# Operand stores of a feed-forward stage begun by GpSimd's queue instead of SyncE's, and one addition per step made on VectorE instead of GpSimd

## The chip, the cores and the metric

The kernel runs on one core of one Trainium2 chip, as one program in one launch. The core has five engines with an instruction queue each: TensorE (PE) multiplies matrices, VectorE (DVE) and ScalarE (ACT) work on elements, GpSimd (POOL) does elementwise work too, and SyncE (SP) does nothing but begin transfers (DMA). A transfer is begun by an instruction in an engine's queue; the queue runs in program order, so an instruction that waits holds up all that stands behind it in the same queue. The metric is the device time of one execution in microseconds (us), as a median of runs.

## What is computed

The reference is one layer of a decoder over a sequence of 1024 rows of 1024 values, all in float32: an attention and gating mixer with its output projection, a layer norm, and then a feed-forward stage with a second layer norm. The change touches the feed-forward stage alone:

```python
x = layer_norm(ALPHA * x + (1 + g1) * y, ln1_g, ln1_b)       # y: the mixer's output
h = x * (1 + sc2) + sh2                                      # 1024 x 1024
f = (jax.nn.silu(h @ w1) * (h @ w3)) @ w2                    # w1, w3: 1024 x 2816, w2: 2816 x 1024
return layer_norm(ALPHA * x + (1 + g2) * f, ln2_g, ln2_b)
```

## The kernel before

A float32 factor is split into a high part in a rounded format and the rest, the low part: ACT writes the high part (L102; the program calls such tiles wH), and DVE subtracts it from the factor for the low part (L107, wL). Each product of two factors is then three matmuls (high·high, high·low, low·high), issued by `prod` at L1106 in the up stage and at L1333 in the down stage.

**The up stage** makes silu(h@w1)·(h@w3). It uses a scheme that gets a 2×2 block product out of seven products instead of eight, at the price of sums of blocks. It has 22 steps, one for each of 11 pairs of column blocks p and each of the two matrices (w = 0 for w1, 1 for w3). Before a step, `prep1` and `prep2` load two 512-KB pieces of the weight (`raw`, from a pool of four buffers that the pieces of w2 share), build the sums `sa` and `sb` on DVE (L1080 to L1088) and split piece and sums into wH and wL. A step itself is `up_first` (bank pa, its result copied to a tile pt by ACT at L1155), `up_second` (pa goes on), and `up_rest` (banks pb and pcd). In `up_rest` DVE adds pb to the first product (L1175), ACT copies a bank to p5 (L1178), GpSimd adds the first product to it (L1179), and DVE adds the three other banks (L1183, L1187, L1190).

**What is stored.** The down stage needs 77 operand blocks of 128×1024, `comb[i, p]` for seven products i = P1 to P7 and 11 p. They are built during the up stage and go through device memory. The left half comes from `act_out`: h·silu (L1132) and its sums `as` (L1139 to L1146). The right half comes from `w2_sums`: two pieces of w2 are loaded (w2r), four sums are made on DVE (L1047 to L1050, tiles wt), and four of them stored. Each store is one call of `put`, a DMA of 128×512 elements (256 KB). There are 121: 44 of wt, 44 of as, 30 of h and 3 of ea, which are early h. Eleven times, w2_sums runs once every two steps, so that its four puts come in one bunch.

**The down stage** (from about 1008 us) loads the blocks back (`cr`, L1225 and L1226), splits them and multiplies (L1333). Beside that it prepares the residual: the rows r come from device memory (L1290), two vectors lag and lab are loaded as 128×1024 tiles, GpSimd scales each once (L1260, L1262), and DVE makes r·lag (L1294) and adds lab (L1273) for each of eight row tiles.

**What sets the order.** All loads and stores of this stage are issued by SP. The order of the instructions in every queue is laid out ahead of the run by a scheduler, from a model of durations. Tiles wH, sa, sb, wt, as and others come out of one pool of 41 buffers (`B`), nearly all of which long-lived operands hold in this stage. So a new wH gets the buffer of a tile that has just been done with, and where that tile is the source of a put, wH waits until the put has landed. A DMA further waits for the one that was eight before it on the same semaphore lanes (eight lanes for SP's DMAs).

Of the kernel before, what the change touches and what calls it, by code (L numbers as in the profile page):

```python
# [14 lines left out]
MULT, ADD, SUB = ALU.mult, ALU.add, ALU.subtract  # L15
# [28 lines left out]
def hymba_kernel(ctx, tc, x, c, w_ada, b_ada, w_in, cmp_pos, cmp_w1, cmp_w2, vn_g, vn_b, w_s, b_s,  # L44
# [4 lines left out]
    V_, P_, A_ = nc.vector, nc.gpsimd, nc.scalar  # L49
    dma = nc.sync.dma_start  # L50
# [21 lines left out]
    def H2(dt=F32, tag="h2"):  # L72
        return sml.tile([128, 512], dt, tag=tag, name=nm_(tag), bufs=NPT if tag == "pt" else 4)

    def G(nm="g"):
        return psg.tile([128, 512], F32, tag="g", name=nm_(nm), bufs=3)

    def S2(nm="s"):
        return pss.tile([128, 2, 512], F32, tag="s", name=nm_(nm))
# [445 lines left out]
    for a in range(2):  # L525
        p = G("pws")
# [434 lines left out]
    for n in range(NC_ + TL):  # L961
# [26 lines left out]
        while eq and (n >= eq[0][0] or n == NC_ + TL - 1):  # L988
            _, i, kv = eq.pop(0)
# [39 lines left out]
    comb = {(i, p): dram.tile([128, 1024], F32, name=f"comb{i}_{p}") for i in DN for p in range(NP)}  # L1029

    def put(i, p, side, src):

        dma(comb[i, p][:, side * 512:side * 512 + 512], src)

    def w2_blk(p, z):
        return w2[(2 * p + z) * 128:(2 * p + z + 1) * 128]
# [3 lines left out]
    def w2_sums(p):  # L1040

        rw = [RAW("w2r") for _ in range(2)]
        for z in range(2):
            load(rw[z], w2_blk(p, z), 8)
        (b11, b12), (b21, b22) = [halves(r) for r in rw]
        (t1, t3), (t2, t4) = halves(B("wt")), halves(B("wt"))
        V_.tensor_tensor(t1, b12, b11, SUB)  # L1047
        V_.tensor_tensor(t3, b22, b12, SUB)
        V_.tensor_tensor(t2, b22, t1, SUB)
        V_.tensor_tensor(t4, b21, t2, SUB)  # L1050
        for i, b in zip(("P4", "P5", "P6", "P7"), (t4, t1, t2, t3)):
            put(i, p, 1, b)
# [48 lines left out]
    def prod(o, a, b, start=True, early=False):  # L1101

        for i in range(4):
            (lh, ll), (rh, rl) = a[i], b[i]
            for n, (x_, y_) in enumerate(((lh, rh), (lh, rl), (ll, rh))):
                r = nc.tensor.matmul(o, x_, y_, start=start and i == 0 and n == 0, stop=i == 3 and n == 2, skip_group_check=not start)  # L1106
                if early:
                    in_order(r)
            if early:
                ticks[0] += 1  # L1110
                if ticks[0] in TR:
                    advance_h2()
        marks.append(r)
# [11 lines left out]
    def act_out(p, w, q, c):  # L1125

        if w == 0:
            s = silu[p, q] = room(p, q)
            A_.activation(s, c, AF.Silu)
        else:  # L1130
            s = silu.pop((p, q))
            V_.tensor_tensor(s, s, c, MULT)  # L1132
            a = acts.setdefault(p, {})
            a[q] = s
            if q != 1:
                put({0: "P1", 2: "P2", 3: "P4"}[q], p, 0, s)
            if q == 1:
                (s1, s3), (s2, s4) = a["s"] = halves(B("as")), halves(B("as"))
                V_.tensor_tensor(s1, a[1], a[3], ADD)  # L1139
                V_.tensor_tensor(s3, a[0], a[1], SUB)  # L1140
                V_.tensor_tensor(s2, s1, a[0], SUB)
                for i, t in (("P5", s1), ("P6", s2), ("P7", s3)):
                    put(i, p, 0, t)
            if q in (1, 2) and 2 in a and "s" in a:
                _, (s2, s4) = a["s"]
                V_.tensor_tensor(s4, a[2], s2, SUB)  # L1146
                put("P3", p, 0, s4)
# [10 lines left out]
    def up_second(p, w, a, early=False):  # L1158
        prod(a, ops[p, w]["A12"], BOP["B21"], False, early)
        act_out(p, w, 0, a)  # L1160
# [8 lines left out]
    def up_rest(p, w, a):  # L1169
        o, p1 = ops[p, w], keep.pop((p, w))  # L1170
        b = (OT if (2 * p + w) % 2 else G)("pb")
        cd = S2("pcd")
        c, d = cd[:, 0, :], cd[:, 1, :]
        prod(b, o["S2"], BOP["T2"])
        V_.tensor_tensor(p1, p1, b, ADD)  # L1175
        prod(c, o["S1"], BOP["T1"])
        p5 = H2(F32, "pt")
        A_.activation(p5, c, AF.Copy)  # L1178
        P_.tensor_tensor(p5, p5, p1, ADD)  # L1179
        if a is not None:  # L1180
            up_second(p, w, a)
        prod(d, o["S3"], BOP["T3"])
        V_.tensor_tensor(p5, p5, d, ADD)  # L1183
        act_out(p, w, 3, p5)
        prod(c, o["S4"], BOP["B22"], False)
        p7 = H2(F32, "pt")
        V_.tensor_tensor(p7, p1, c, ADD)  # L1187
        act_out(p, w, 1, p7)
        prod(d, o["A22"], BOP["T4"], False)
        V_.tensor_tensor(p1, p1, d, ADD)  # L1190
        act_out(p, w, 2, p1)
# [51 lines left out]
    for n, s in enumerate(steps):  # L1243
        if n < 2:
            continue
        if n + 1 < len(steps):
            if n + 1 >= NE:
                prep1(*steps[n + 1])
            prep2(*steps[n + 1])
        if n in W2:  # L1250
            w2_sums(W2[n])
        if n == len(steps) - 1:
            down_start()
        up_rest(*s, up_first(*s) if n >= NE else None)
# [182 lines left out]
```

## Time and profile before

| what | before |
|---|---|
| median of three runs | 1239.02 us (1238.83 to 1240.66) |
| profiled execution, its own time | 1242.85 us |
| span in its profile | 1241.1 us |
| mean granted clock of TensorE in the span | 0.994 |
| TensorE busy | 1201.1 us (97%) |
| VectorE busy | 951.0 us (77%) |
| ScalarE busy | 555.3 us (45%) |
| GpSimd busy | 246.9 us (20%) |

The median is compared with the median of the changed kernel; the rows come from the one profiled execution, which was 3.83 us longer than the median and has 1.75 us outside its span. Rows of a timeline give start, duration, engine, line, operation, output<-input and shape; in square brackets stands the idle time of the engine before the instruction and what ended it. SPq is SP issuing a DMA. "x2" says that two instructions in a row were joined in one line of the answer. The granted clock (PEclk) is a share of TensorE's full speed.

### The profile page before, as it was taken

Reading aid. Unit: us, or ns where it says so; the run is one execution under the profiler, and the core shown is the slowest. Engines: PE = TensorE matmul, PEld = TensorE weight load, DVE = VectorE, ACT = ScalarE, POOL = GpSimd, SP = SyncE. Lnnn points to the kernel's source line nnn. Section 1 sums busy time; section 2 is a strip of 40 time slices with the busy share of each in tenths; the row PEclk is TensorE's granted clock in tenths of the full one; section 3 lists DMA queues with packets and bytes.
Section 4 is the critical chain, followed back from the end, with each engine's and each line's share of the span. In section 5 each row is a group of like instructions: output and inputs, shape, how many; then the busy total and the mean of one; then the engine's idle time right before and its main releaser. Section 6 shows DMA issues by size and latency. Waiting matters only on the chain.

```text
span 1241.1 us, 16779 instructions
## 1 busy us (share of the span) xinstructions
PE 1201.1 (97%) x5908; PEld 1000.4 (81%) x5908; DVE 951.0 (77%) x1696; ACT 555.3 (45%) x1023; POOL 246.9 (20%) x277
## 2 busy tenths in 40 slices
PE   7999999999999999999989899999999999999996
PEld 5888888888888888888868788888788877888885
DVE  6568798599889997867587577776667759877886
ACT  5653223398889995044333233232322323453420
POOL 0022026075556673100001100000010000000011
PEclk9999999999999999999999999999999999999999
DMA  9624549110000006534053555546544469786741
GB/s 351 245 59 124 164 118 260 48 69 1 2 1 2 1 2 219 161 130 134 28 176 104 153 165 157 162 130 240 163 153 150 134 224 344 232 279 208 240 148 68
DMA packets 125690, 178.35 MB, mean 144 GB/s; under 512 B 16420, under 2 KB 74916, under 8 KB 125607
## 3 DMA queue, kind: packets, MB, share of 16 engines
q1 hardware_dynamic: 125606, 177.30, 44.6%
q8 instruction: 46, 0.75, 0.3%
q14 instruction: 38, 0.30, 0.1%
HBM read 135.06 MB, written 40.11 MB: 141 GB/s over the span
## 4 chain that ended last, share of the span: by engine, by line
PE 87%; DVE 7%; DMA 2%; issue 2%; ACT 1%; POOL 0%; DVEq 0%; ACTq 0%; POOLq 0%
PE pcd L1106 17%; PE pa L1106 10%; PE px L1333 8%; PE py L1333 7%; PE pt L128 4%; PE pb L1106 4%; PE ps L730 2%; PE ps L732 2%; PE pwo L92 2%; PE pwo L96 2%; PE pwo L95 2%; PE ot L774 2%; PE ot L773 2%; PE pv L92 1%; PE pv L95 1%
## 5 line engine op out<-in xcount | busy, mean ns | idle before, releaser
L102 ACT ACTIVATE wH<-cr 128x1024 fp32r<-128x1024 f32 x77 | 81.5, 1061 | 115.4 <-DMA cr<-combP 48.9
L743 POOL TENSOR_SCALAR P<-P,ast,gate 128x640 f32<-128x640 f32 (+7 forms) x128 | 99.5, 784 | 66.6 <-DVE ast L742 43.0
L107 DVE TENSOR_TENSOR wL<-cr,wH 128x1024 fp32r<-128x1024 f32 x77 | 94.0, 1233 | 23.7 <-ACT wH L102 23.0
L1179 POOL TENSOR_TENSOR pt<-pt,pt 128x512 f32<-128x512 f32 x20 | 30.9, 1545 | 396.6 <-ACT pt L1178 191.0
L107 DVE TENSOR_TENSOR pt<-pt,pt 128x512 fp32r<-128x512 f32 (+1 forms) x148 | 99.8, 682 | 7.1 <-ACT pt L102 6.3
L676 ACT ACTIVATE P<-P,ast 128x640 f32<-128x640 f32 (+7 forms) x128 | 93.9, 735 | 2.0 <-DVE ast L675 1.5
L102 ACT ACTIVATE pt<-pt 128x512 fp32r<-128x512 f32 (+1 forms) x148 | 87.2, 592 | 16.2 <-PE pt L128 13.5
L1106 PE MATMUL pa<-h2H,wH 128*128 128x512 f32 x192 | 77.0, 401 | 5.3 <-ACT wH L102 5.3
L102 ACT ACTIVATE wH<-raw 128x1024 fp32r<-128x1024 f32 (+2 forms) x43 | 44.5, 1040 | 81.3 <-DMA combP<-wt 69.7
L128 PE MATMUL pt<-ident,P 128*128 128x128 f32 x528 | 79.0, 272 | 0.2 <-DVE pt L107 0.2
L1106 PE MATMUL pa<-h2L,wH 128*128 128x512 f32 x192 | 76.2, 397 | 0.0
L1106 PE MATMUL pa<-h2H,wL 128*128 128x512 f32 x192 | 75.8, 395 | 0.0
L128 PEld LDWEIGHTS pt<-ident,P 128*128 128x128 f32 x528 | 65.0, 140 | 12.9 <-issue 0.5
L107 DVE TENSOR_TENSOR wL<-raw,wH 128x1024 fp32r<-128x1024 f32 (+2 forms) x43 | 51.4, 1199 | 30.9 <-ACT wH L102 29.0
L1333 PE MATMUL px<-wH 128*128 128x512 f32 x176 | 68.4, 395 | 3.1 <-DVE h L1406 2.2
L1333 PE MATMUL px<-wL,wH 128*128 128x512 f32 x176 | 69.3, 394 | 1.8 <-DVE wL L107 1.8
L1106 PE MATMUL pcd<-wH,wH 128*128 128x512 f32 x176 | 68.8, 391 | 1.5 <-DVE h L1132 0.8
L1333 PE MATMUL px<-wH,wL 128*128 128x512 f32 x176 | 69.3, 394 | 0.0
L1106 PE MATMUL pcd<-wL,wH 128*128 128x512 f32 x176 | 68.5, 389 | 0.0
L1106 PE MATMUL pcd<-wH,wL 128*128 128x512 f32 x176 | 68.5, 389 | 0.0
L773 PE MATMUL ot<-pt,V 128*128 128x512 f32 x132 | 59.8, 453 | 0.0
L730 PE MATMUL ps<-KH,Q 128*128 128x512 f32 (+2 forms) x192 | 57.2, 354 | 1.0 <-DVE ast L675 0.9
(300 smaller groups left out, 3396.9 us busy)
## 6 DMA issues: line engine op xcount, KB each, us to landing
raw<-in_w SPq DMA_DIRECT2D x46, 512.0 KB, 5.6
cr<-combP SPq DMA_DIRECT2D x44, 512.0 KB, 4.4
ada<-in_w_adaT SPq DMA_DIRECT2D x32, 512.0 KB, 6.1
w2r<-in_w SPq DMA_DIRECT2D x22, 512.0 KB, 4.3
combP<-wt SPq DMA_DIRECT2D x44, 256.0 KB, 5.2
combP<-as SPq DMA_DIRECT2D x44, 256.0 KB, 2.1
cr<-combP SPq DMA_DIRECT2D x33, 256.0 KB, 4.5
cr<-in_w SPq DMA_DIRECT2D x33, 256.0 KB, 5.0
```

Of the source, the lines that this page charges most:

```text
L92: a = nc.tensor.matmul(o, lh[0], rh[0], start=start, stop=False)
L95: nc.tensor.matmul(o, lh[0], rh[1], start=False, stop=False)
L102: A_.activation(o, i, AF.Copy)
L107: return V_.tensor_tensor(o, i, f(h), SUB)
L128: nc.tensor.transpose(out=p[:, j * 128:(j + 1) * 128], in_=src(j), identity=ident)
L676: A_.activation(P, P, AF.Exp, scale=-1.0, bias=nm, accum_out=den)
L730: nc.tensor.matmul(o, Q(h, hf)[:, qs], KH(br - 1, kv, kf)[:, ks], start=True, stop=False)
L743: P_.tensor_scalar(P, P, st[:, 2, hh:hh + 1], gcol(i, h, br), MULT, MULT)
L773: nc.tensor.matmul(ot, vs, hl[0], start=False, stop=False)
L1106: r = nc.tensor.matmul(o, x_, y_, start=start and i == 0 and n == 0, stop=i == 3 and n == 2, skip_group_check=not start)
L1179: P_.tensor_tensor(p5, p5, p1, ADD)
L1333: lastm[0] = nc.tensor.matmul(o, x_[:, ts_], y_[:, 512:1024], start=not cont and p == 0 and n == 0, stop=p == NP - 1 and n == 2, skip_grou ...
```

## The change

Two lines change. In `put` all 121 stores are begun by GpSimd's queue instead of SP's. In `up_rest` the addition at L1179 is done by DVE: 20 instructions, one for each of the 20 steps that use `up_rest`.

```diff
     def put(i, p, side, src):
 
-        dma(comb[i, p][:, side * 512:side * 512 + 512], src)
+        P_.dma_start(comb[i, p][:, side * 512:side * 512 + 512], src)
...
         p5 = H2(F32, "pt")
         A_.activation(p5, c, AF.Copy)
-        P_.tensor_tensor(p5, p5, p1, ADD)
+        V_.tensor_tensor(p5, p5, p1, ADD)
         if a is not None:
             up_second(p, w, a)
```

(`dma` is SP's `dma_start`, P_ is GpSimd, V_ is DVE.) GpSimd's DMAs get eight semaphore lanes of their own (DMASW; SP's are DMAHW). As the scheduler lays the queues out anew and buffers are handed out in another order, instructions move on all engines. Three places are shown. Numbers behind tile names tell instances apart.

ACT at the end of the step before p = 2, where TensorE idles at 686 to 690 us in the trace; in brackets are the semaphores on which an instruction waits. wH_7080 is the high part of the next step's first piece. Before:

```order
L102 ACTIVATE wH_6946<-sa_6942 128x1024 [waits DVE_49]
L102 ACTIVATE wH_6952<-sb_6943 128x1024 [waits DMAHW4_49,DMAHW5_49,DVE_49,Activation_49]
L102 ACTIVATE w_6956<-raw_6940 128x512 [waits DMAHW2_49,DMAHW3_49,DMAHW0_49,Activation_49]
L1129 ACTIVATE h_7045<-pt_7015 128x512 [waits DMAHW3_49,DVE_49]
L102 ACTIVATE wH_7080<-raw_7078 128x1024 [waits DMAHW3_49,DMAHW0_49,DMAHW4_49,DVE_49,Activation_49]
L1155 ACTIVATE pt_7116<-pa_7103 128x512 [waits PE_49]
```

And now:

```order
L102 ACTIVATE wH_6946<-sa_6942 128x1024 [waits DVE_49]
L102 ACTIVATE wH_6952<-sb_6943 128x1024 [waits DVE_49,PE_49]
L1129 ACTIVATE h_7045<-pt_7015 128x512 [waits DMASW4_49,DVE_49]
L102 ACTIVATE w_6956<-raw_6940 128x512 [waits DMASW1_49,DMAHW4_49,DMASW0_49,Activation_49]
L102 ACTIVATE wH_7080<-raw_7078 128x1024 [waits DMAHW7_49,PE_49]
L1155 ACTIVATE pt_7116<-pa_7103 128x512
```

Before, wH_7080 waited for two puts of wt (lanes 3 and 4), whose source had its buffer; now it has another buffer and waits for its own raw piece (lane 7) and a past product. The same holds at the step before p = 7, where TensorE idles at 882 to 884 us. At both places the first product with this wH also stands 12 matmuls later in TensorE's queue than before.

TensorE at the step before p = 3, which stands for six alike (it is at 732 us in the trace): pa_7539 is the next step's first bank, pcd_7272 a bank of the step that is ending. Rows with - are the order before, rows with + the order now:

```order
 L1106 MATMUL pcd_7402<-wL_6549,wH_7229 128x512
 L1106 MATMUL pcd_7402<-wH_6548,wL_7230 128x512
+L1106 MATMUL pa_7539<-h2H_5824,wH_7363 128x512
+L1106 MATMUL pa_7539<-h2L_5825,wH_7363 128x512
 L1106 MATMUL pcd_7272<-wH_6563,w_7100 128x512
 L1106 MATMUL pcd_7272<-wL_6564,w_7100 128x512
...
 L1106 MATMUL pcd_7272<-wL_6574,w_7100 128x512
 L1106 MATMUL pcd_7272<-wH_6573,w_7100 128x512
-L1106 MATMUL pa_7539<-h2H_5824,wH_7363 128x512
-L1106 MATMUL pa_7539<-h2L_5825,wH_7363 128x512
```

The first two matmuls of pa now stand ahead of the last 12 matmuls of pcd instead of behind them. Their wH_7363 still gets the buffer of a wt tile and waits for the puts of its two halves, which are GpSimd's first two of the bunch (P5, then P7).

SP at the change to the down stage (about 1006 to 1024 us in the trace); lag, lab and r are the residual's tiles, cr an operand block. Before:

```order
L1226 DMA cr_9572<-in_w 128x512
L1033 DMA combP_10_6195<-h_9308 128x512
L1033 DMA combP_10_6261<-h_9323 128x512
L1033 DMA combP_10_6206<-as_9466 128x512
L86 DMA lag_9499<-in_ln_g 128x1024
L1033 DMA combP_10_6250<-as_9466 128x512
L1033 DMA combP_10_6217<-as_9467 128x512
L86 DMA lab_9500<-in_ln_b 128x1024
L1033 DMA combP_10_6239<-h_9354 128x512
L1290 DMA r_9495<-zspill 128x1024
```

SP now, and GpSimd's queue now at the same place (there the two scalings stood alone before):

```order
L1226 DMA cr_9572<-in_w 128x512
L86 DMA lag_9499<-in_ln_g 128x1024
L86 DMA lab_9500<-in_ln_b 128x1024
L1290 DMA r_9495<-zspill 128x1024
L1290 DMA r_9496<-zspill 128x1024
```

```order
L1033 DMA combP_10_6206<-as_9466 128x512
L1033 DMA combP_10_6250<-as_9466 128x512
L1033 DMA combP_10_6217<-as_9467 128x512
L1260 TENSOR_SCALAR lag_9499<-lag_9499 128x1024
L1033 DMA combP_10_6239<-h_9354 128x512
L1262 TENSOR_SCALAR lab_9500<-lab_9500 128x1024
L1033 DMA combP_10_6228<-as_9467 128x512
```

The loads of lag, lab and r no longer stand behind puts that wait for DVE's results; the two scalings of lag and lab now do.

## Rows read from the trace of the kernel before

**Rows 1.** The page's first part: engine, busy us (share of span), instructions.

```profile
PE 1201.1 (97%) x5908; PEld 1000.4 (81%) x5908; DVE 951.0 (77%) x1696; ACT 555.3 (45%) x1023; POOL 246.9 (20%) x277
```

**Rows 2.** Windows: stretch, us, busy (instructions) of PE/PEld/DVE/ACT/POOL, PEclk, DMA share, GB/s.

```profile
720.00:760.00 40.00, 40.00 (x178) 32.78 (x177) 28.94 (x40) 13.48 (x19) 2.99 (x2) 1.00 0.50 155
```

**Rows 3.** Windows of L1106's matmuls alone: PE, PEld, PEclk, DMA share, GB/s.

```profile
686.17:694.01 7.84, 4.62 (x13) 3.27 (x12) 0.78 0.74 221
881.93:888.40 6.47, 4.41 (x13) 3.10 (x11) 0.74 0.76 205
```

**Rows 4.** The same of L1333's matmuls, after the down stage's start.

```profile
1035.21:1042.10 6.89, 5.08 (x16) 3.70 (x15) 0.75 0.92 341
```

**Rows 5.** Timeline of PE: the four long idle times and one undisturbed step.

```profile
642.74 0.50 PE L1106 MATMUL pcd<-h2H,wH 128*128 128x512 f32 x1 [1.53 <-DVE pt L1183]
...
689.78 0.50 PE L1106 MATMUL pa<-h2H,wH 128*128 128x512 f32 x1 [3.22 <-ACT wH L102]
...
732.12 0.39 PE L1106 MATMUL pcd<-wH,w 128*128 128x512 f32 x1
732.40 0.50 PE L1106 MATMUL pa<-h2H,wH 128*128 128x512 f32 x1
...
884.39 0.50 PE L1106 MATMUL pa<-h2H,wH 128*128 128x512 f32 x1 [2.06 <-ACT wH L102]
...
1037.66 0.50 PE L1333 MATMUL px<-wL,wH 128*128 128x512 f32 x1 [1.81 <-DVE wL L107]
```

**Rows 6.** Waits: engine and line, waited for; total us, times, longest us.

```profile
ACT wH L102 <- DMA combP<-wt: 69.7, 8, 9.4
```

**Rows 7.** Timeline of SP's issues near 680 and 724 us.

```profile
678.53 0.38 SPq L86 DMA_DIRECT2D raw<-in_w  x1
...
723.85 3.53 SPq L1033 DMA_DIRECT2D combP<-wt  x4
```

**Rows 8.** The page's DMA issues: count, KB each, median us from issue to landing.

```profile
raw<-in_w SPq DMA_DIRECT2D x46, 512.0 KB, 5.6
...
combP<-as SPq DMA_DIRECT2D x44, 256.0 KB, 2.1
```

**Rows 9.** Timeline of ACT at the undisturbed step of rows 5.

```profile
731.29 1.06 ACT L102 ACTIVATE wH<-raw 128x1024 fp32r<-128x1024 f32 x1 [9.43 <-DMA combP<-wt]
```

**Rows 10.** Timeline of DVE: the sources of puts P5 and P7.

```profile
723.14 0.68 DVE L1047 TENSOR_TENSOR wt<-w2r 128x512 f32<-128x512 f32 x1
723.74 0.68 DVE L1048 TENSOR_TENSOR wt<-w2r,w2r 128x512 f32<-128x512 f32 x1
```

**Rows 11.** GpSimd by line: count, busy us, mean ns of one, idle before.

```profile
L124 POOL TENSOR_TENSOR st<-st,mhalf 128x16 f32<-128x16 f32 (+1 forms) x16 | 39.9, 2498 | 63.1 <-DVE st L123 62.7 <-DVE ast L742 0.4
L1179 POOL TENSOR_TENSOR pt<-pt,pt 128x512 f32<-128x512 f32 x20 | 30.9, 1545 | 396.6 <-ACT pt L1178 191.0 <-DVE pt L1175 184.3 <-DMA cr<-in_w 21.3
```

**Rows 12.** Timeline of GpSimd: one of its additions.

```profile
638.21 1.52 POOL L1179 TENSOR_TENSOR pt<-pt,pt 128x512 f32<-128x512 f32 x1 [58.92 <-ACT pt L1178]
```

**Rows 13.** Timeline of DVE beside that addition, and beside the last such one.

```profile
638.51 1.77 DVE L1141 TENSOR_TENSOR as<-as,ea 128x512 f32<-128x512 f32 x1
...
982.45 1.78 DVE L1141 TENSOR_TENSOR as<-as,h 128x512 f32<-128x512 f32 x1
```

**Rows 14.** Timeline of SP at the change to the down stage.

```profile
1017.74 0.32 SPq L1033 DMA_DIRECT2D combP<-as  x1
...
1018.63 0.87 SPq L1033 DMA_DIRECT2D combP<-as  x2
...
1021.29 0.83 SPq L1290 DMA_DIRECT2D r<-zspill  x1
```

**Rows 15.** Timeline of DVE at the same place.

```profile
1029.37 1.23 DVE L1294 TENSOR_TENSOR r<-r,lag 128x1024 f32<-128x1024 f32 x1 [2.41 <-DMA r<-zspill]
...
1036.38 1.22 DVE L107 TENSOR_TENSOR wL<-cr,wH 128x1024 fp32r<-128x1024 f32 x1
```

**Rows 16.** Timeline of GpSimd at the same place.

```profile
1023.42 1.34 POOL L1260 TENSOR_SCALAR lag<-lag 128x1024 f32<-128x1024 f32 x1 [16.60 <-DMA combP<-as]
1026.01 1.87 POOL L1262 TENSOR_SCALAR lab<-lab 128x1024 f32<-128x1024 f32 x1 [1.25 <-DMA combP<-h]
```

## The prediction

> **What bounds the kernel now.** I read the page's first part, then the windows of equal stretches, PE's timeline where its busy time falls short, the list of waits, and the timelines of whoever ends a wait. TensorE is busy for 97% of the span [rows 1], so a change that touches no matmul can only give back the remaining idle time, or add to it. In an undisturbed stretch of the up stage PE runs 178 matmuls in 40 us [rows 2], one per 0.225 us. The reader is to see in [rows 5] four places in the feed-forward stage where it doesn't: it waits 3.22 and 2.06 us for a wH of ACT, 1.81 us for a wL of DVE after the change to the down stage, and 1.53 us for DVE's addition at 642.74. After the first three the clock is lower for a while: over 686.17 to 694.01 us the granted clock is 0.78, over 881.93 to 888.40 it is 0.74 [rows 3], over 1035.21 to 1042.10 it is 0.75 [rows 4], each a mean of time at 2.4 GHz and at 1.2 GHz. What each stretch cost in all is its length less its matmuls at 0.225 us: 7.84 − 13 × 0.225 = 4.9 us, 6.47 − 13 × 0.225 = 3.55 us, 6.89 − 16 × 0.225 = 3.3 us. These stretches and the fourth place are what can be won.
>
> Why wH is late: ACT waits eight times, 69.7 us in all, for a put of wt to land before it may write wH [rows 6], because wH gets the buffer of the put's source. Two of the eight are the stalls at 689.78 and 884.39. In the other six, of which the step at 732 us is one, ACT waits longer, up to 9.4 us, but PE still has work until wH is there: at 731.29 ACT starts wH [rows 9], and 1.11 us later, at 732.40, PE begins with it, 0.28 us after the matmul before it [rows 5]. It is just in time.
>
> **The change part by part.**
> *The two stalls for wH.* At both, wH now has a buffer that no put holds and waits for its raw piece. That piece is issued at 678.53 [rows 7]; at the median of 5.6 us to landing [rows 8] it is there at 684.1. PE had work until 686.4 before (686.17, the start of the stretch, and one matmul), and now has 12 matmuls more, 2.7 us, so until 689.1; wH must start 1.1 us before that, at 688.0. The piece has 3.9 us to spare, and the past product that wH waits for ends 16 matmuls ahead of pa in the new order, 3.6 us. Both stretches go: −4.9 and −3.55.
>
> *The wL at 1037.66.* It stood on DVE behind four pairs of residual instructions, which started 2.41 us late because r had not landed [rows 15]. r was issued at 1021.29 behind puts that waited for DVE [rows 14]; now it goes out some 14 us earlier. Then wL starts at 1036.38 − 2.41 = 1033.97 and ends at 1035.20, before PE runs dry at 1035.66 (1035.21, the start of the stretch in [rows 4], and two matmuls). −3.3, if lag and lab are ready too. Their scalings now stand in GpSimd's queue behind puts. With an issue price q for a put on GpSimd, three puts from 1017.74 on end at 1017.74 + 3q; then lag takes 1.34, a put q, and lab 1.87 [rows 16]. With q = 1.55 lab is done at 1027.2; DVE wants it at 1029.37 − 2.41 + 1.23 = 1028.2. With q = 2.5 it is done at 1030.95, 2.8 us late, and nothing is won.
>
> *What a put on GpSimd costs.* No DMA of GpSimd is in this trace. The nearest rows: an issue on SP takes 0.32 us [rows 14], GpSimd's addition on a tile of the same size 1.55 us, and the longest group of GpSimd instructions 2.50 us [rows 11]. I take q = 1.55, since it is the same engine with a tile of this size, and keep 0.32 and 2.5 as ends. 121 puts at 1.55 are 188 us of GpSimd's time in the up stage, where it has only the additions to do; that itself is hidden.
>
> *The new wait at six steps.* There PE now wants wH 12 matmuls earlier, at 732.40 − 2.70 = 729.70, so ACT must start it at 728.6. It still waits for the puts P5 and P7, whose sources DVE has ready at 723.82 and 724.42 [rows 10]. SP began its four puts at 723.85 [rows 7], at once, and P7 landed only at 731.29, 6.9 us after its source was ready, because in SP's queue it lay behind raw pieces. A put of `as` lands 2.1 us after its issue began [rows 8], 1.8 us after an issue of 0.32 ended. From GpSimd's queue, with q = 1.55, P7 is issued by 723.82 + 3.10 = 726.92 and lands at 728.7, 0.1 us late: six times 0.1 is +0.6. With q = 0.32 it costs nothing; with q = 2.5 P7 lands at 730.6, 2.0 us late, six times +12. The Trainium skill, DMA: Bandwidth & Descriptors, § Specifications, gives about 1 us to the first byte of a DMA from GpSimd, 0.6 us from SP; no run here shows it. By it, P7 would land 0.4 us later and the six would cost an estimated +2.4 more.
>
> *The addition on DVE.* GpSimd's addition of 638.21 to 639.73 [rows 12] overlaps DVE's addition at 638.51, which takes 1.77 us [rows 13] instead of the 0.68 us of others with the same shape [rows 10]. The timeline shows 11 such pairs, the last at 982.45 [rows 13], in 20 additions [rows 11], so DVE now loses 11 × 1.1 = 12 us and will instead do 20 × 0.6 = 12 us more (0.60 us from start to start [rows 10]). DVE's sum is unchanged. At 642.74, where PE waits for DVE, 1.1 us go and 0.6 us come: −0.5.
>
> *Queues.* SP loses 121 instructions, some of which waited for DVE; the loads behind them go out sooner, into DMA engines that are half idle (share 0.50 in [rows 2]). GpSimd's queue has only puts and, at its end, the residual's scalings: what a waiting put holds up there is other puts. As the order changes on every engine, I allow for two new gaps of half the 1.53 us at 642.74: +1.5.
>
> *Sum:* −4.9 − 3.55 − 3.3 − 0.5 + 0.6 + 1.5 = −10.15. Profiled execution: 1242.85 − 10.15 = 1232.7. It lies 3.83 us above the median of the runs, so the median should become 1228.9; I say 1229.0.
>
> **The rivals.**
> *A, slower: the six steps pay.* If puts from GpSimd land as late as they do now (6.9 us after the source), ACT starts wH at 731.29 instead of 728.6. PE then idles 2.7 us, between the two stalls of 2.06 and 3.22, after which the clock fell; with the slow matmuls each place costs between 3.55 and 4.9, say 4.1 us. Six are 24.6 us: 1229.0 − 0.6 + 24.6 = 1253. With q = 2.5 the six cost 12 and the boundary wins nothing: 1229.0 − 0.6 + 12 + 3.3 = 1243.7. It decides from 1.8 us lost at each place on, that is P7 at 730.4, 6.0 us after its source, as 10.75 us are won elsewhere. For it: the margin is nil, and the raw pieces are in flight at just that time. Against: the lateness of today comes from lying behind 512-KB pieces in one queue, the DMA engines are half idle, and puts with nothing ahead land in 2.1 us. The Trainium skill, DMA: Bandwidth & Descriptors, § Issuing engines are not separate DMA queues, speaks for A: it says that DMAs of all issuing engines run on the same 16 DMA engines and interleave, so that another issuer only saves issuing time. By that rule P7 would land about when it does now, and the time would be A's 1253; no row of before can tell, since all its puts and pieces come from one queue. Chance 0.14, two thirds of it for the smaller price.
>
> *B: the gain is half.* A stall goes and the next engine is late: DVE is busy 77% of the span, and wL follows wH on it. If one of the two wH stalls stays in half and the wL stall stays whole, 1229.0 + 2 + 3.3 = 1234.3. For it: DVE has the residual, the splits and one more kind of addition in one queue. Chance 0.14.
>
> *C, no change: the waits only move.* Wherever a wH no longer waits for a put, some other tile got that buffer; if it is wanted as early as wH was, the 10 us come back at a third place. 1239. For it: 41 buffers, nearly all held. Against: at the two places it is now the wH of sums that wait for puts, and PE wants those only for pb and pcd, at least 12 matmuls after pa's first. Chance 0.10. That the change does nothing of what it says is excluded by the order, which shows wH without a put's semaphore at both stalls.
>
> **How the numbers follow.** Forecast 0.62 (its own range 1226 to 1231: the costs of 2.1 taken at none or at twice that, and 1 us less if other short gaps shrink), B 0.14, C 0.10, A 0.14. A measurement of this kernel can tell about 0.2%, 2.5 us. Faster by more than that: forecast and B, 0.76. Within it: C, and the edge of A, 0.11. Slower: A's rest, 0.13. The range that should hold 8 in 10 reaches from 1224 to 1240: it takes in B and C, and the lower end allows for gaps of the up stage that close as well; A lies outside.
>
> **What would show it.** In the new profile PE's timeline should have no idle time over 1 us at the first matmul of pa with wH before p = 2 and p = 7, with the granted clock at 1.00 there; no waits of ACT's wH for a put of wt with idle PE behind it; r landed before DVE wants it, and no wL wait after the change to the down stage; DVE's additions all near 0.68 us. The six steps decide: if PE waits there for wH, the put's landing minus the end of L1048 says how long a put on GpSimd takes, and above 6.0 us the change is slower.

## The result, and the profile after

The changed kernel takes 1247.47 us as a median of four runs (1245.78 to 1251.24), the kernel before 1238.92 us in the same comparison: a ratio of 1.0064 (95% interval 1.0046 to 1.0081). It is 0.6% slower, where 0.8% faster was forecast. The profiled execution took 1251.24 us with a span of 1249.5 us, so it too lies 3.8 us above its median, and the two profiles can be set side by side: 8.4 us more in the span.

TensorE's timeline, in the same columns as [rows 5], shows where:

```profile
643.28 0.50 PE L1106 MATMUL pcd<-h2H,wH 128*128 128x512 f32 x1 [1.08 <-DVE pt L1183]
...
727.80 0.50 PE L1106 MATMUL pa<-h2H,wH 128*128 128x512 f32 x1 [2.20 <-ACT wH L102]
...
769.72 0.77 PE L1106 MATMUL pa<-h2H,wH 128*128 128x512 f32 x1 [1.96 <-ACT wH L102]
...
811.88 0.50 PE L1106 MATMUL pa<-h2H,wH 128*128 128x512 f32 x1 [2.20 <-ACT wH L102]
...
929.62 0.50 PE L1106 MATMUL pa<-h2H,wH 128*128 128x512 f32 x1 [2.61 <-ACT wH L102]
...
972.47 0.50 PE L1106 MATMUL pa<-h2H,wH 128*128 128x512 f32 x1 [2.84 <-ACT wH L102]
...
1012.45 0.50 PE L1106 MATMUL pa<-h2H,wH 128*128 128x512 f32 x1 [1.58 <-ACT pt L1155]
```

The two stalls of before at p = 2 and p = 7 are gone, the wL wait after the change to the down stage is gone, and the wait for DVE's addition is 1.08 us instead of 1.53. In their place stand five stalls of the same kind as the two, at p = 3, 4, 5, 8 and 9, and one of 1.58 us at p = 10, where ACT copies pa late because a wH of the down stage, which waits for its load, stands before the copy. The five are exactly the places where the first bank pa has moved ahead of the last 12 matmuls. The section on the change has six of them; at p = 6 pa stands where it stood, and wH has a buffer that no store holds. So of the eight wH that waited for a wt store before (p = 2 to 9) five are left. ACT's row in the list of waits (total, times, longest), which answers to [rows 6], says the same:

```profile
ACT wH L102 <- DMA combP<-wt: 44.4, 5, 9.3
```

The windows of L1106's matmuls over the five stretches (columns as in [rows 3]):

```profile
725.21:732.00 6.79, 4.59 (x14) 3.35 (x13) 0.77 0.47 159
767.37:774.00 6.63, 4.67 (x14) 3.45 (x13) 0.74 0.50 165
809.29:815.00 5.71, 3.51 (x16) 2.57 (x15) 1.00 0.61 204
926.62:933.00 6.38, 3.77 (x11) 2.73 (x10) 0.78 0.51 168
969.25:976.00 6.75, 3.91 (x17) 2.92 (x16) 1.00 0.53 176
```

In three of the stretches the clock was a mix of 2.4 and 1.2 GHz after the idle time, in two it stayed at 2.4 GHz. Length less matmuls at 0.225 us gives 3.6, 3.5, 2.1, 3.9 and 2.9 us, 16 us together; this is a little low, since a matmul that a window cuts counts as a whole one. Both profiles have 5908 matmuls of TensorE, so one can also compare the times at which the same number of them has started. By that count the five places cost 3.9, 3.8, 2.5, 4.6 and 3.1 us, 17.9 together, p = 10 costs 1.9 and p = 6 0.2. Won are 4.8 us at p = 2, 3.6 at p = 7, 3.9 at the change to the down stage and 0.4 at the addition, 12.7 together. Another 1.0 us arose in the first 141 us, which the change does not touch (the granted clock over 120 to 140 us is 0.91, before 1.00). Together these are 8.3 of the 8.4 us.

Why the store lands late is seen at p = 3. GpSimd's issues there, and then SP's:

```profile
719.69 1.14 POOL L1033 DMA_DIRECT2D combP<-wt  x2 [2.47 <-DVE wt L1047]
721.68 0.54 POOL L1033 DMA_DIRECT2D combP<-wt  x1 [0.85 <-DVE wt L1049]
722.41 0.54 POOL L1033 DMA_DIRECT2D combP<-wt  x1 [0.19 <-issue]
```

```profile
718.82 3.69 SPq L86 DMA_DIRECT2D raw<-in_w  x3
```

P5 is issued 0.6 us earlier than P7, which goes out at about 720.3, as soon as DVE has made it. ACT gets its buffer at 726.69:

```profile
726.69 1.06 ACT L102 ACTIVATE wH<-raw 128x1024 fp32r<-128x1024 f32 x1 [8.71 <-DMA combP<-wt]
```

That is 6.4 us after P7's issue and 6.7 us after its source was ready at 720.00, although nothing stands ahead of P7 in GpSimd's queue but P5. SP, which has no stores left, issues three raw pieces of 512 KB between 718.8 and 722.5. The window of 6.2 us from P7's issue on shows the DMA engines full (share 1.02, 331 GB/s), in columns as in [rows 2]:

```profile
720.30:726.50 6.20, 5.29 (x24) 4.05 (x22) 2.07 (x3) 0.00 (x0) 1.61 (x3) 1.00 1.02 331
```

The page's DMA issues give 6.0 us to landing as the median of the 44 wt stores and 2.6 of the as stores, which mostly meet no piece ([rows 8] has 2.1 for as before):

```profile
combP<-wt POOLq DMA_DIRECT2D x44, 256.0 KB, 6.0
combP<-as POOLq DMA_DIRECT2D x44, 256.0 KB, 2.6
```

What DVE does is as forecast. By line, over the feed-forward stage, the additions beside the former GpSimd ones are down from 1.78 us to 0.68, and the 20 new ones cost 13.7 us; DVE's busy time is 951.0 us in both profiles:

```profile
L1179 DVE TENSOR_TENSOR pt<-pt,pt 128x512 f32<-128x512 f32 x20 | 13.7, 684 | 0.1
...
L1141 DVE TENSOR_TENSOR as<-as,h 128x512 f32<-128x512 f32 x9 | 6.2, 684 | 0.0
```

### The profile page after: what moved, and what is told of

It reads as the page before. It is cut to its first block, busy times and chain, and to the rows that moved or that the text cites. A ratio compares the mean times of both kernels' runs of the same rounds, so it can differ in the third digit from the quotient of the medians.

```text
span 1249.5 us, 16795 instructions
## 1 busy us (share of the span) xinstructions
PE 1203.1 (96%) x5908; PEld 999.9 (80%) x5908; DVE 951.0 (76%) x1716; ACT 556.2 (45%) x1023; POOL 279.1 (22%) x378
## 4 chain that ended last, share of the span: by engine, by line
PE 62%; issue 24%; DVE 7%; POOL 4%; ACT 1%; DMA 1%; POOLq 0%; DVEq 0%; SPq 0%; ACTq 0%
PE px L1333 9%; PE py L1333 7%; PE pt L128 4%; POOL combP L1033 4%; PE pa L1106 4%; PE pcd L1106 3%; PE ps L730 2%; PE ps L732 2%; PE pwo L92 2%; PE pwo L95 2%; PE pwo L96 2%; PE ot L774 2%; PE ot L773 2%; PE pv L92 1%; PE pv L95 1%
## 5 line engine op out<-in xcount | busy, mean ns | idle before, releaser
L1106 PE MATMUL pa<-h2H,wH 128*128 128x512 f32 x192 | 76.0, 396 | 13.4 <-ACT wH L102 11.8
L1187 DVE TENSOR_TENSOR pt<-pt,pcd 128x512 f32<-128x512 f32 x20 | 13.7, 687 | 83.7 <-PE pcd L1106 83.7
L1106 PE MATMUL pa<-h2L,wH 128*128 128x512 f32 x192 | 75.0, 391 | 0.0
L1106 PE MATMUL pa<-h2H,wL 128*128 128x512 f32 x192 | 74.7, 389 | 0.0
L1333 PE MATMUL px<-wH 128*128 128x512 f32 x176 | 68.1, 392 | 2.9 <-DVE h L1406 2.2
L1106 PE MATMUL pcd<-wH,wH 128*128 128x512 f32 x176 | 68.7, 390 | 1.5 <-DVE h L1132 0.8
L1333 PE MATMUL px<-wL,wH 128*128 128x512 f32 x176 | 68.6, 390 | 0.0
L1333 PE MATMUL px<-wH,wL 128*128 128x512 f32 x176 | 68.5, 389 | 0.0
L1106 PE MATMUL pcd<-wL,wH 128*128 128x512 f32 x176 | 68.5, 389 | 0.0
L1106 PE MATMUL pcd<-wH,wL 128*128 128x512 f32 x176 | 68.5, 389 | 0.0
L1033 POOL DMA_DIRECT2D combP<-h x30 | 16.2, 542 | 187.9 <-DVE h L1132 187.8
```

The lines of the kernel that those rows point to most:

```text
L1033: P_.dma_start(comb[i, p][:, side * 512:side * 512 + 512], src)
L1333: lastm[0] = nc.tensor.matmul(o, x_[:, ts_], y_[:, 512:1024], start=not cont and p == 0 and n == 0, stop=p == NP - 1 and n == 2, skip_grou ...
```

## The experiments

Each was compared with the kernel before in the same session. "Landing" is the page's median from issue to landing of the 44 wt stores, as far as the trace shows their landing (in e4 and e8 their source is w2r); "idle" is the time that TensorE waits at pa for wH, from the list of waits. Both are of the one profiled execution. The scheduler lays out every kernel anew, so each edit also moves other instructions; where that bears on a reading it is said.

| kernel | us | ratio (95% interval) | landing | idle (places) |
|---|---|---|---|---|
| before | 1238.9 to 1241.4 | 1 | 5.2 | 5.3 (2) |
| the change | 1247.5 | 1.0064 (1.0046 to 1.0081) | 6.0 | 11.8 (5) |
| e1 stores only | 1241.4 | 1.0005 (0.9992 to 1.0019) | 6.5 | 7.8 (2) |
| e2 addition only | 1231.5 | 0.9920 (0.9905 to 0.9936) | 2.7 | none |
| e3 first bank last | 1287.4 | 1.0373 (1.0352 to 1.0394) | 6.3 | none |
| e4 change, sums in place | 1227.5 | 0.9889 (0.9872 to 0.9905) | 2.8 | none |
| e5 as e2, piece first | 1240.0 | 1.0003 (0.9989 to 1.0017) | 4.8 | 4.3 (5) |
| e6 change, wt on SyncE | 1233.0 | 0.9940 (0.9919 to 0.9960) | 3.5 | none |
| e7 change, pieces held | 1239.3 | 0.9994 (0.9982 to 1.0006) | 2.7 | none |
| e8 addition, sums in place | 1229.0 | 0.9912 (0.9888 to 0.9935) | 2.2 | none |
| e9 as e7, from second bunch | 1230.4 | 0.9928 (0.9913 to 0.9943) | 2.8 | none |
| e10 before, pieces after stores | 1231.8 | 0.9934 (0.9922 to 0.9947) | 2.7 | none |
| e11 change, only wt on GpSimd | 1255.5 | 1.0129 (1.0096 to 1.0163) | 6.2 | 15.0 (5) |

My first theory was that the order costs (theory O below): a stall stands wherever pa is early and its wH waits for a store. The rival was that GpSimd's queue is slow in itself (theory Q).

**e1, e2: one part each.** e1 is the change without the second hunk of its diff, e2 the change without the first.

> Only the stores move to GpSimd's queue; the addition stays on GpSimd. Theory O (order): what costs is that TensorE's first bank of a step stands ahead of the last 12 matmuls of the step before while its wH waits for a wt store. In this kernel that is so at two places, as in the kernel before (after: five), and each costs about 3.6 us. The wL stall at the change to the down stage (3.3 us) goes. So 1239 - 3.3 = about 1236 us, with idle TensorE over 1.5 us at the two places p = 2 and p = 7 only. Theory Q (queue): stores from GpSimd are themselves what is late, and they cost wherever a buffer waits for one: about 1247 us, as the whole change.

> Only the addition moves to VectorE; the stores stay on SyncE. In this kernel eight steps have the first bank ahead of the 12 matmuls and a wH that waits for a wt store. Theory O: six more places than before at 3.6 us, less 0.5 us at the addition of the step at 640 us: 1239 + 21 = about 1260 us. Theory Q: the stores are where they were, so no change: 1238.5 us.

The stores alone change nothing measurable, the addition alone makes the kernel 0.8% faster. Both theories missed. e2 has the early first bank at eight steps with a wH behind a wt store, and no stall at all; so an early bank behind a store is not enough. SP's issues at p = 3 in e2, and ACT's wait there:

```profile
718.29 0.92 SPq L1033 DMA_DIRECT2D combP<-wt  x2
719.26 0.45 SPq L86 DMA_DIRECT2D raw<-in_w  x1
720.09 1.04 SPq L1033 DMA_DIRECT2D combP<-wt  x2
721.23 1.70 SPq L86 DMA_DIRECT2D raw<-in_w  x2
```

```profile
721.38 1.06 ACT L102 ACTIVATE wH<-raw 128x1024 fp32r<-128x1024 f32 x1 [3.94 <-DMA combP<-wt]
```

P5 and P7 stand ahead of the raw piece in the queue, and the buffer is free 2.5 us after P7's issue. In the kernel before, a piece stood right ahead of the two stores, and it took 6.8 us:

```profile
723.25 0.38 SPq L86 DMA_DIRECT2D raw<-in_w  x1
```

(the stores' row, 0.6 us later, is in [rows 7]). The cleanest pair is p = 2 and p = 7: there pa stands as early in e2 as in the kernel before, and wH has the buffer of the same wt tile, but P7 lands 2.6 and 2.75 us after its issue instead of 5.9 and 5.6. The median of P5 and P7 at p = 2, before and in e2:

```profile
combP<-wt SPq DMA_DIRECT2D x2, 256.0 KB, 5.4
...
combP<-wt SPq DMA_DIRECT2D x2, 256.0 KB, 2.3
```

The two stalls of e1 are longer than before (3.79 and 3.96 us), as its P7 lands 6.1 and 7.1 us after its issue. That costs 1.7 us more at each of the two places and eats what is won at the change to the down stage, where the wL wait is gone as forecast:

```profile
690.25 0.79 PE L1106 MATMUL pa<-h2H,wH 128*128 128x512 f32 x1 [3.79 <-ACT wH L102]
...
887.67 0.80 PE L1106 MATMUL pa<-h2H,wH 128*128 128x512 f32 x1 [3.96 <-ACT wH L102]
```

**e3: the whole change with the first bank kept last.**

```diff
-    def prod(o, a, b, start=True, early=False):
+    tail = [None]
+
+    def prod(o, a, b, start=True, early=False, after=None):
...
+                if after is not None and i == 0 and n == 0:
+                    order(r, after)
...
-        prod(a, o["A11"], BOP["B11"], True, early)
+        prod(a, o["A11"], BOP["B11"], True, early, tail[0])
...
         prod(d, o["A22"], BOP["T4"], False)
+        tail[0] = marks[-1]
```

> The whole change, and in addition the first matmul of a step's first bank is kept behind the last matmul of the step before (an ordering edge without a wait), so no place has the early first bank, while seven wH still wait for wt stores on GpSimd's queue. Theory O: the five stalls (17.9 us together in the profile of the change) go: 1247.5 - 17.9 = about 1229.5 us. Theory Q: stores land 6 us after their issue all the same and the stalls stay or come back within 12 matmuls (2.7 us): 1240 to 1247 us.

It is 3.7% slower, far from either. The 12 matmuls of the last bank wait for DVE to read the bank before them, and the next step's pa was the work that covered that wait; without it TensorE stands at every step:

```profile
PE pcd L1108 <- DVE pt L1191: 30.1, 19, 4.5
PE pcd L1108 <- DVE pt L1187: 8.3, 10, 1.1
```

The stalls for wH did go, but as every step now comes later, that says nothing for or against theory O. What e3 shows is that an order that looks like the place of a stall can be what hides another.

**e4: the whole change with w2's sums in place.** No tile of the pool is a store's source for wt any more.

```diff
-        (t1, t3), (t2, t4) = halves(B("wt")), halves(B("wt"))
+        t1, t3, t4, t2 = b11, b12, b21, b22
```

> The whole change, and the four sums of w2 are written over the loaded pieces instead of into tiles of the pool, so no wH gets the buffer of a fresh wt store; the order has the early first bank at eight steps. Theory O in its second half (early bank and a fresh store are both needed): no stall for wH, about 1229 us. Rival: the pieces' four buffers are now held until the stores land, some 6 us longer, the raw pieces go out later, and TensorE waits for them: 1240 us or more.

1227.5 us, the fastest of all, 1.1% faster than before, with every store on GpSimd. It removes the shared buffer, and it also holds the next pieces, whose four buffers are now the stores' source: the stores land in 2.8 us. So a store from GpSimd is not slow in itself, and theory Q fell. The wL wait after the change to the down stage is gone here too.

After these four runs the theory was B, the burst: what a store takes is set by the raw pieces that are in flight with it on the DMA engines, and the queues matter only in that one queue keeps pieces behind stores and two queues don't.

**e5: as e2, with the piece put first again.**

```diff
+        d = dma(comb[i, p][:, side * 512:side * 512 + 512], src)
+        if side and i in ("P5", "P7"):
+            lastput.append(d)
...
+        if lastput:
+            behind.append(d)
+            if len(behind) == 2:
+                for u in lastput:
+                    order(u, d)
```

(In the second part d is a raw piece's load; the second one after w2's sums goes ahead of the stores P5 and P7.)

> As the kernel with the addition alone on VectorE (1231.5 us, where the two wt stores P5 and P7 stand on SyncE ahead of the next raw piece and land in 2.0 to 2.7 us), but with that raw piece put ahead of the two stores in the same queue. Theory B (burst): a store's time to landing is set by the raw pieces already in flight on the DMA engines; P7 then lands some 6 us after its source and TensorE waits at the six steps that have an early first bank and a wH behind the store, 6 x 3.6 us: about 1253 us. Rival: what made the addition alone faster is the rest of its order, and the place of two stores in a queue changes little: 1232 us.

Some 8 us slower than e2, as slow as before. At six of the eight places (not p = 2 and p = 7) pa is as early and wH behind the same wt store as in e2, so there little but the place of two issues in one queue differs. Direction and landing (4.9 to 5.5 us for P7) are theory B's, the size is not: TensorE waits at five places for 4.3 us in all, 0.4 to 1.1 us each, and its clock stays up, where I had put 3.6 us from stalls twice as long. By the count of matmuls 7.7 of the 8.0 us between the two profiles lie at p = 2 to 10, 1.3 to 1.5 us each at p = 3, 4 and 5 and 0.4 to 1.0 at the others; p = 2 and p = 7, where the order differs, have 0.8 of them.

```profile
765.03 0.50 PE L1117 MATMUL pa<-h2H,wH 128*128 128x512 f32 x1 [1.14 <-ACT wH L102]
```

**e6 and e11: the stores divided between the queues**, both with the addition on DVE. The edit in `put` is `(dma if side else P_.dma_start)` for e6 and `(P_.dma_start if side else dma)` for e11.

> The whole change, but the 44 wt stores go back to SyncE; the 77 others stay on GpSimd. All eight steps have the early first bank with a wH behind a wt store, and P5 and P7 stand ahead of the next raw piece in SyncE's queue. Theory B: P7 lands in 2 to 3 us and no step waits; the loads of the residual go out early as well: 1229 to 1231 us. Rival (it is the early bank and the shared buffer alone): eight stalls, about 1255 us.

> The complement of the kernel with wt stores on SyncE: the addition on VectorE, the 44 wt stores on GpSimd, the 77 others on SyncE. TensorE's order has the early first bank at the same five steps as the whole change. Theory B: the 44 stores alone make the loss, P7 lands 6 us after its source: about 1247 us. Rival (121 stores together make it): half way, 1238 to 1241 us.

The 44 wt stores decide and the 77 others do not: with wt on SyncE there is no stall, with wt alone on GpSimd there are all five. At these five places pa is early and wH behind the same wt store in e6 as in the whole change; what differs is when the stores land. The median of P5 and P7 at p = 3, in the change and in e6:

```profile
combP<-wt POOLq DMA_DIRECT2D x2, 256.0 KB, 5.4
...
combP<-wt SPq DMA_DIRECT2D x2, 256.0 KB, 2.2
```

e6 ends 2 us above the range that was expected, and no faster than e2, although the wL wait is gone as expected. e11 is 8 us slower than the whole change and than was expected; its stalls are longer, as at p = 3:

```profile
728.61 0.66 PE L1106 MATMUL pa<-h2H,wH 128*128 128x512 f32 x1 [3.04 <-ACT wH L102]
```

They are longer by what P7 lands later (7.05 us after its issue at p = 3, 6.2 in the change). At p = 5 and p = 9 the idle time is 3.12 and 3.09 us and the granted clock falls, which it did not in the change; these two places make 5.4 of the 6.4 us between the two profiles:

```profile
809.97:817.00 7.03, 3.92 (x11) 3.14 (x12) 0.80 0.48 160
...
972.50:982.00 9.50, 6.41 (x17) 5.03 (x17) 0.64 0.38 129
```

Why P7 lands later there stays open.

**e7 and e9: the whole change, but a raw piece waits until P7 has landed.**

```diff
-        P_.dma_start(comb[i, p][:, side * 512:side * 512 + 512], src)
+        d = P_.dma_start(comb[i, p][:, side * 512:side * 512 + 512], src)
+        if side and i == "P7":
+            lastput[0] = d
...
+        if lastput[0] is not None:
+            tc.add_manual_dep(d.ins, lastput[0].ins.name, SYNC, reason="hold")
```

(e9 has `if side and i == "P7" and p:`, which leaves out the first bunch. In the second part d is a raw piece's load.)

> The whole change, all stores on GpSimd, but the first raw piece behind each bunch of wt stores waits on SyncE until the store P7 has landed, so that no piece is in flight beside P5 and P7. Theory B: P7 lands in 2.6 us instead of 6.2 and the five stalls go; the pieces go out some 3 us later, which may cost up to 1 us a step: 1229 to 1240 us. Rival (GpSimd's stores are slow in themselves): P7 still 5 to 6 us, 1245 us or more.

> As the kernel with the raw pieces held behind store P7, but not at the first bunch, where the held piece was wanted at once and TensorE idled 8.3 us at 630 us. Theory B: the five stalls stay away and the 8.3 us go as well: 1239.3 - 8 = about 1231 us, though all stores stay on GpSimd and the addition on VectorE. Rival (the hold only moved the loss to the start): the wait comes back at the second bunch, 1239 us.

For the landing this is the direct test: same queues, same engine for the addition, and the pieces out of the way. GpSimd's issues at p = 3 in e7, and SP's:

```profile
726.18 1.74 POOL L1036 DMA_DIRECT2D combP<-wt  x3 [2.47 <-DVE wt L1052]
...
728.11 0.54 POOL L1036 DMA_DIRECT2D combP<-wt  x1 [0.19 <-issue]
```

```profile
729.52 5.02 SPq L87 DMA_DIRECT2D raw<-in_w  x4
```

P7, the second of the three, goes out at 726.8 and SP is released at 729.5: under 2.8 us instead of 6.4. It is so at all ten bunches that raw pieces follow: P7 lands in 2.5 to 2.65 us. All five stalls are gone. The order of the other instructions changed too (at those steps pa now stands 36 matmuls later than in the change), so the landing is what this run shows by itself, and the time only together with e6. e7 as a whole stays at 1239.3 us, because at the first bunch a held piece is wanted at once:

```profile
638.97 0.80 PE L1113 MATMUL pb<-wH,wH 128*128 128x512 f32 x1 [8.12 <-ACT wH L103]
```

Without the hold at that one place e9 reaches 1230.4 us, about the 8 us that were expected, and 17 us better than the change. pa stands as late in it as in e7.

**e8: the addition on DVE, stores on SyncE, sums in place.** The edits are those of e2 and e4.

> The addition on VectorE, all stores on SyncE, and w2's sums written over the loaded pieces. Neither half of the stall is there (no wH behind a fresh wt store, stores ahead of the pieces). If the wt stores are all there is between the versions, it ends where the whole change with sums in place did, 1227.5 us, less or more the wL wait after the change to the down stage that early loads of the residual save (1.7 us): 1227 to 1230 us. Rival: stores on SyncE hold up the raw pieces that wait behind them, 1235 us.

As expected, and not to be told from e4, whose interval overlaps. Of what is left, e8 still has the wL wait after the change to the down stage (1.6 us), and e4 has not, which is the one place where stores on GpSimd do what they were forecast to do.

**e10: the kernel before with one ordering edge.** Stores on SyncE, addition on GpSimd.

```diff
+        if side and i == "P7" and p:
+            lastput[0] = d
...
+        if lastput[0] is not None:
+            order(d, lastput[0])
```

> The kernel before (stores on SyncE, addition on GpSimd) with one ordering edge: from the second bunch on, a raw piece stands behind the wt store P7 in SyncE's queue. Theory B: P7 lands in 2 to 3 us instead of 5.6 to 6.7 and the two stalls of before (9.0 us together) go: 1239.9 - 9.0 = about 1231 us, as with the addition alone on VectorE. Rival (the addition's engine is what made that kernel faster): 1239 to 1240 us.

1231.8 us: an edge that moves no work to any engine gives 8.4 us, where the addition on DVE gave 9.9 in e2, and P7 lands in 2.4 to 2.75 us from the second to the tenth bunch. So the gain does not need the addition on another engine. That the landing alone gave it is not shown by e10: with the edge pa also stands 12 matmuls later than before at p = 2 and p = 7, and 24 later at the six other places. e2 shows it for p = 2 and p = 7, where pa stayed as early as before.

## Why the prediction was wrong, point by point

- **The two stalls and the wL wait** went, as forecast, and so did 0.45 us at the addition; DVE's sum stayed the same to 0.1 us. 12.7 us were won, where the prediction has 12.25.
- **The step that failed** is "The new wait at six steps": that P7, once it no longer lies behind raw pieces in SP's queue, lands 2.1 us after its issue began, at 728.7, 0.1 us late. Its buffer came free 6.4 us after its issue, and five places that were to cost 0.1 us each cost 17.9 us together. The sign that the prediction names came true: 6.7 us from the end of P7's source, above 6.0, and a slower kernel. The store of 2.1 us was taken from as stores, which meet few pieces; a store with nothing ahead of it in its own queue still shares the DMA engines with pieces from another. e7 measures the difference with the queue held the same: 2.7 us against 6.0 as medians.
- **The number that misled** was the DMA share of 0.50 in [rows 2]. It is a mean over 40 us, and from it the prediction argued that the DMA engines are half idle. Over the 6.3 us in which the stores of before were under way the share is 0.95:

```profile
725.00:731.30 6.30, 6.30 (x30) 5.21 (x29) 2.07 (x3) 0.01 (x1) 0.00 (x0) 1.00 0.95 295
```

  A stretch as long as the wait that was in question would have shown ahead of time that they are not. It would not have told the landing by itself: while P7 lands in 2.6 us in e7 and 2.4 us in e2, the share is 0.75 and 0.82, with the stores' own transfers in it.
- **The rival A was the case, with its mechanism.** P7 lands 6.2 us after its issue beside SP's pieces and 2.6 us without them, from the same queue of GpSimd. The rule of the Trainium skill, DMA: Bandwidth & Descriptors, § Issuing engines are not separate DMA queues, that DMAs of all issuing engines interleave on the same 16 DMA engines, is what these runs show: in the change, over 719 to 727 us, packets of GpSimd's queue take 38% and packets of SP's 58% of the 16 DMA engines' time. A had said that ACT gets the buffer 6.9 us after P7's source, and it was 6.7. A chance of 0.14, and only a third of it for this branch of A, was too little. A's price was too high, 1253 us against 1247.5: five places instead of six, and 3.6 us a place instead of 4.1. At the three places where the clock fell the price was right (3.9, 3.8 and 4.6 us); at the two that kept 2.4 GHz it was 2.5 and 3.1. The sixth place was miscounted: in the new order three of the eight steps, not two, have a wH without a store.
- **The price of an issue** was taken at 1.55 us; it is 0.54. With the price right and the landing free of pieces the six steps would have cost nothing, so this error decided nothing.
- **Not seen at all** was the place of the stores in the one queue. SP's queue did two things: it put the stores behind a piece in the kernel before, and it kept the next pieces behind the stores. The change takes away both; e2 and e5 show that the first alone could be had by order, for 8 to 10 us.
- **At the boundary** the mechanism held. r goes out at 1017.65, earlier than before, although TensorE is 12.2 us later there. The scalings stand behind stores, as feared, but end at 1033.0 and 1036.75, ahead of the first r·lag. That starts at 1039.49, right behind four wL as before, and no longer waits for r. So the next wL starts at 1046.30; less the 12.2 us that is 1034.1, where the prediction had 1033.97 and the kernel before 1036.38:

```profile
1017.65 2.10 SPq L1290 DMA_DIRECT2D r<-zspill  x3
```

```profile
1037.21 2.35 DVE L107 TENSOR_TENSOR wL<-cr,wH 128x1024 fp32r<-128x1024 f32 x2
1039.49 2.35 DVE L1294 TENSOR_TENSOR r<-r,lag 128x1024 f32<-128x1024 f32 x2
...
1046.30 1.21 DVE L107 TENSOR_TENSOR wL<-cr,wH 128x1024 fp32r<-128x1024 f32 x1
```

- **What stays open:** why P7 lands later in e11 than in the whole change, and how the gain of e9 and e10 divides between the early landing and the later place of pa.

## What to carry to other kernels

A store that frees a buffer is late by the loads that are in flight with it, whichever queue they come from (here 2.6 us without and 6.2 us with two or three 512-KB loads); putting it in another queue takes it out from behind the loads in program order but not off the DMA engines, and it lets the loads go that its own queue would have held. Where such a store is wanted soon, put it ahead of the bulk loads (e2, e6), hold the loads for the 2 to 3 us it needs (e9), or take the buffer out of the chain (e4). And read the DMA share over a window as long as the wait, not over a stage.

## What the runs showed of the hardware

- A store of 256 KB issued by GpSimd holds that engine for 0.54 us (SP: 0.32 us) and lands in 2.6 us where few loads are in flight, SP's in 2.1 (medians of the as stores). P7 lands in 2.5 to 2.65 us in ten bunches of e7, with no piece of a weight in flight, and in 5.75 us in the eleventh, beside loads of the down stage; in the change it takes 4.75 to 6.9 us.
- Of five idle times between 1.96 and 2.84 us in one execution three were followed by a lower granted clock (0.74 to 0.78 in the windows above) and two were not (2.20 and 2.84 us, 1.00), so the length of the idle time alone did not decide.
- An addition of two SBUF tiles on DVE took 1.77 us beside GpSimd's own addition and 0.68 us with GpSimd only issuing DMAs.
